# Two-layer decoder trunk on one core: the first FFN product in seven block products in place of eight, and layer 1's modulation vectors at other places

## The chip, the cores and the metric

The kernel runs on one core of a Trainium2 chip. The metric is the device time of one execution in microseconds (us); lower is better. One core has a matmul engine (TensorE, PE in the profile), two vector engines (VectorE or DVE, GpSimd or POOL), an activation engine (ScalarE, ACT), a sync engine (SyncE, SP) that here only issues transfers, and 16 DMA engines that move data between the chip's memory and the on-chip buffers.

## The reference, cut to what matters

```python
cond = jax.nn.silu(c)                                  # c: 1 x 1024
for layer in range(2):
    mod = cond @ ada_w[layer] + ada_b[layer]           # 1024 x 6144
    sh1, sc1, g1, sh2, sc2, g2 = jnp.split(mod, 6, axis=-1)
    h = modulate(rms_norm(x, mix_norm[layer]), sh1, sc1)
    y = ab_mixer(h, ...) if layer == 0 else cd_mixer(h, ...)
    x = x + g1[:, None, :] * y
    h = modulate(rms_norm(x, ffn_norm[layer]), sh2, sc2)
    gate, up = jnp.split(h @ w1[layer], 2, axis=-1)    # w1: 1024 x 5632
    x = x + g2[:, None, :] * ((silu(gate) * up) @ w2[layer])    # w2: 2816 x 1024
```

x has 512 tokens of 1024 features. The six modulation vectors of a layer (1024 numbers each) are numbered s0 to s5 in the kernel, in the order of the split; `ada_w` holds 4 MB for each. They don't depend on x, so they can be made at any time before they are used.

## The kernel before, in words

**Precision.** Every big product takes both operands as a sum of a rounded part hi and a rest lo and makes three matmuls, hi·hi, hi·lo, lo·hi (`mm3`, L119 to L122). `split` (L115) makes hi on ACT (L116) and lo on DVE (L117); in the mixers `lo_eng` may set lo on POOL.

**FFN, first product (`ffn`, L1226).** The 5632 columns of w1 are 22 gate tiles and 22 up tiles of 128 columns. For each i from 2 to 21 PE multiplies gate tile i and up tile i with all 512 tokens (8 row blocks × 3 matmuls of 128x512 each, called f), then `glu` (L1233) makes silu on ACT and the product g on DVE. Tiles 0 and 1 are multiplied earlier in `ffn_first` (L1205) in halves of 256 tokens. Weights come in 1 MB transfers into `rawp` (two buffers of 1 MB), 256 columns at a time (`load_cols`).

**FFN, second product.** For each i from 0 to 21, `kt(i)` (L1243) splits one tile of w2 (128x1024, two tiles per 1 MB transfer, `load_rows`, L410) and one tile of g; then PE makes 24 matmuls of 128x512 (called w) into the eight PSUM banks. The last four i's are made per block of 128 tokens, each followed by its gated residual.

**Modulation.** There are three ways to make a vector. `ada_strip` (L227): PE multiplies strips of `ada_w` with cond and `ada_cols` (L242) turns the row into columns. `ada_vec` (L255): 1 MB transfers into `adap` (one buffer of 1 MB), and DVE accumulates them with cond as a per-partition scalar, four operations on 128x512 per transfer (L217, L219). `ada_pair` (L278): the same for two vectors at once, 64 partitions each, in two transfers of 0.5 MB (L289), accumulated at L295 and L297 and finished by `pair_fin` (L299). In layer 0's first product the kernel makes s5 of layer 0, the pair s0, s1 of layer 1 and s2 of layer 1, one step for each i (`side`, `next(side, None)`); in layer 0's second product it makes the pair s3, s4 of layer 1, one step for every second i (`side2`). Each step issues the next transfer and accumulates the one issued a step before. Layer 1's first product makes s5 of layer 1. `gate_bcast` (L338) spreads a gate vector over all partitions by PE; for the FFN it stands at the end of the first product.

**Order.** PE, ACT, DVE and POOL execute in the order in which the code is written (`manual_schedule` with `MANUAL`); SP issues its transfers in program order, each when its buffer is free. In the mixers, generators are interleaved step by step by `run` (L517). In layer 1's mixer `in_cd` loads w_in with `load_cols` (L397) and `load_rows` (L410) into the two `rawp` buffers.

Of the kernel before, what the change touches and what calls it, by code (L numbers as in the profile page):

```python
# [69 lines left out]
def trunk(ctx, tc, x, c, positions, ada_w, ada_b, ffn_w1, ffn_w2, ab_w_in, gla_gate_up,  # L70
# [9 lines left out]
    adap = ctx.enter_context(tc.tile_pool(name="adap", bufs=1))  # L80
# [22 lines left out]
    def small(w=1, name="t"):  # L103
        return tiny.tile([P, w], F32, tag=f"t{w}", name=nm(name))

# [97 lines left out]
    def ada_acc(dst, rt, q, E):  # L203
        if E is G:
            r3 = rt.rearrange("p (j n) -> p j n", j=4)
            E.tensor_tensor(r3, r3, cond[:, 4 * q:4 * q + 4].unsqueeze(2).to_broadcast([P, 4, 512]), op=ALU.mult)
            E.tensor_tensor(rt[:, 0:1024], rt[:, 0:1024], rt[:, 1024:2048], op=ALU.add)
            if q:
                E.tensor_tensor(dst, dst, rt[:, 0:512], op=ALU.add)
                E.tensor_tensor(dst, dst, rt[:, 512:1024], op=ALU.add)  # L210
            else:
                E.tensor_tensor(dst, rt[:, 0:512], rt[:, 512:1024], op=ALU.add)
            return
        for j in range(4):
            r, c_ = rt[:, j * 512:(j + 1) * 512], cond[:, 4 * q + j:4 * q + j + 1]
            if q + j == 0:
                E.tensor_scalar(dst, r, c_, None, ALU.mult)  # L217
            else:
                E.scalar_tensor_tensor(dst, r, c_, dst, ALU.mult, ALU.add)  # L219

# [6 lines left out]
    def ada_strip(l, s, acc2, lag):  # L227
        src = ada_w[l].rearrange("(p j) n -> p j n", j=8)
        for n in range(2):
            acc = slot(name="acc")  # L230
            for q in range(2):
                rt = adap.tile([P, 2048], F32, tag="ada", name=nm("ada")).rearrange("p (j n) -> p j n", j=8)
                c0 = s * D + n * 512 + q * 256
                tc.keep_in_program_order(nc.sync.dma_start(rt, src[:, :, c0:c0 + 256]))
                for _ in range(lag):
                    yield
                ps = bank("ad")
                ada_mm(ps[:, 0:256], [rt[:, j] for j in range(8)], 0, 8)
                act(acc[:, q * 256:(q + 1) * 256], ps[:, 0:256], AF.Copy)
            acc2.append(acc)  # L240
# [14 lines left out]
    def ada_vec(l, s, acc2, E, lag):  # L255
        for n in range(2):
            acc2.append(slot(name="acc"))
            if s in (2, 5):
                b = slot(w=512, name="abrow")
                nc.scalar.dma_start(b[0:1], ada_b[l:l + 1, s * D + n * 512:s * D + (n + 1) * 512])  # L260
            for q in range(2):
                c0 = s * D + n * 512
                rt = adap.tile([P, 2048], F32, tag="ada", name=nm("ada"))
                ld = nc.sync.dma_start(
                    rt.rearrange("p (j n) -> p j n", j=4),
                    ada_w[l].rearrange("(p j) n -> p j n", j=8)[:, 4 * q:4 * q + 4, c0:c0 + 512])
                tc.keep_in_program_order(ld)
                for _ in range(lag):
                    yield
                ada_acc(acc2[n], rt, q, E)  # L270
            if s in (2, 5):
                E.tensor_tensor(acc2[n][0:1], acc2[n][0:1], b[0:1], op=ALU.add)
                hi, lo = slot(F32R, name="acchi"), slot(F32R, name="acclo")
                E.tensor_copy(hi, acc2[n])
                E.tensor_tensor(lo, acc2[n], hi, op=ALU.subtract)
                acc2[n] = hi, lo

    def ada_pair(l, s0, acc2):  # L278

        src = ada_w[l].rearrange("(p j) n -> p j n", j=16)  # L280
        for n in range(2):
            dst = slot(name="acc")
            acc2.append(dst)
            for q in range(4):
                rt = adap.tile([P, 2048], F32, tag="ada", name=nm("ada"))
                r3 = rt.rearrange("p (j n) -> p j n", j=4)
                for v in range(2):
                    c0 = (s0 + v) * D + n * 512
                    ld = nc.sync.dma_start(r3[64 * v:64 * v + 64], src[:, 4 * q:4 * q + 4, c0:c0 + 512])  # L289
                    tc.keep_in_program_order(ld)  # L290
                yield
                for j in range(4):
                    c_ = cond2[:, 4 * q + j:4 * q + j + 1]
                    if q + j == 0:
                        V.tensor_scalar(dst, r3[:, j], c_, None, ALU.mult)  # L295
                    else:
                        V.scalar_tensor_tensor(dst, r3[:, j], c_, dst, ALU.mult, ALU.add)  # L297
# [13 lines left out]
    def after(g, n, fn):  # L311
        for i, _ in enumerate(g):
            if i == n:
                fn()
            yield

# [4 lines left out]

    def ada_seq(l, ss, store, fin, E=None, lag=1):
        prev = []
        for s in ss:
            store[s] = []
            for i, _ in enumerate(ada_vec(l, s, store[s], E or V, lag)):
                if i == 2:
                    for q in prev:
                        ada_fin(l, q, store[q])
                    prev = []  # L330
                yield
            if fin and s not in (2, 5):
                prev = [s]
        if prev:
            yield
            ada_fin(l, prev[0], store[prev[0]])
# [1241 lines left out]
```

## Time and profile before

| quantity | value |
|---|---|
| three runs | 1246.60, 1246.76, 1250.62 us; median 1246.76 |
| profiled execution | 1251.88 us, its span 1250.1 us, mean granted clock 0.99 |
| busy over the span | PE 98%, DVE 55%, ACT 38%, POOL 12% |
| chain that ended last | PE 90%, DVE 5%, ACT 2%, issue 2% |
| layer 0, first product, tiles 2 to 21 | about 360.2 to 579.8 us |
| layer 0, second product, i from 0 to 17 | about 580.7 to 678.7 us |
| layer 1, mixer with its output product | about 709 to 881 us |

The span is the time from the first to the last recorded instruction; the profiled execution took 1.78 us more, and 5.12 us more than the median of the runs. The chain follows the end of the kernel back from releaser to releaser; its shares add up to the span. A granted clock of 1.00 in a stretch is 2.4 GHz.

### The profile page before, as it was taken

The numbers are of one execution on the slowest core, as the hardware profiler recorded it, in microseconds if no ns is written. First come the engines' busy times: TensorE is split into PE (matmuls) and PEld (weight loads), VectorE is DVE, ScalarE is ACT, GpSimd is POOL, SyncE is SP. The second block draws the span as 40 slices with busy tenths as digits, with TensorE's granted clock in tenths as the row PEclk, the third lists the DMA queues.
The fourth block names the chain that finished last, engine by engine and source line by source line (L and its number), as shares of the span: only waits on it lengthen the run. The fifth ranks groups of instructions, "written<-read, shape, count | busy, mean of one in ns | idle before, by whom it ended". The sixth has DMA issues, their size and how long they took to land.

```text
span 1250.1 us, 15248 instructions
## 1 busy us (share of the span) xinstructions
PE 1221.9 (98%) x5999; PEld 994.0 (80%) x6000; DVE 693.2 (55%) x1197; ACT 472.5 (38%) x917; POOL 153.0 (12%) x153
## 2 busy tenths in 40 slices
PE   7998999999999999999999999999999999999998
PEld 3776767878888888888888888787988888888886
DVE  4477789657744555654564727866736322224334
ACT  4356337645442122223222565643522222223330
POOL 2043135500100000000000174230100000000000
PEclk8998999999999999999999999999999999999999
DMA  9544554321144686736773123122335332432211
GB/s 314 202 135 134 174 169 136 117 103 40 39 159 135 190 214 162 237 116 185 200 197 114 68 68 110 34 68 68 102 109 195 97 105 69 134 101 101 101 68 68
DMA packets 106804, 160.62 MB, mean 128 GB/s; under 512 B 5334, under 2 KB 67814, under 8 KB 106732
## 3 DMA queue, kind: packets, MB, share of 16 engines
q1 hardware_dynamic: 104704, 158.71, 40.1%
q10 hardware_dynamic: 1964, 0.93, 0.3%
q8 instruction: 47, 0.77, 0.3%
q14 instruction: 25, 0.20, 0.1%
q0 software_dynamic: 64, 0.01, 0.0%
HBM read 157.53 MB, written 2.10 MB: 128 GB/s over the span
## 4 chain that ended last, share of the span: by engine, by line
PE 90%; DVE 5%; ACT 2%; issue 2%; DMA 1%; POOL 1%; ACTq 0%; SPq 0%; POOLq 0%; DVEq 0%
PE f L120 16%; PE f L121 16%; PE f L122 16%; PE w L121 6%; PE w L122 6%; PE w L120 6%; PE op L121 2%; PE op L122 2%; PE op L120 2%; PE ad L225 2%; PE f L128 1%; PE f L129 1%; PE f L131 1%; PE tp L378 1%; PE ko L647 1%
## 5 line engine op out<-in xcount | busy, mean ns | idle before, releaser
L116 ACT ACTIVATE whi<-raw 128x1024 fp32r<-128x1024 f32 x188 | 197.9, 1059 | 375.3 <-PE w L122 134.0
L120 PE MATMUL f<-hhi,whi 128*128 128x512 f32 (+1 forms) x704 | 267.3, 380 | 0.0
L121 PE MATMUL f<-hlo,whi 128*128 128x512 f32 (+1 forms) x704 | 267.2, 380 | 0.0
L122 PE MATMUL f<-hhi,wlo 128*128 128x512 f32 (+1 forms) x704 | 267.2, 380 | 0.0
L117 DVE TENSOR_TENSOR wlo<-raw,whi 128x1024 fp32r<-128x1024 f32 x148 | 178.0, 1222 | 137.0 <-ACT whi L116 136.9
L1236 DVE TENSOR_TENSOR g<-silu,f 128x512 f32<-128x512 f32 x44 | 30.3, 688 | 237.3 <-PE f L122 235.9
L120 PEld LDWEIGHTS f<-hhi,whi 128*128 128x128 f32 x704 | 132.5, 188 | 25.0
L122 PEld LDWEIGHTS f<-hhi,wlo 128*128 128x128 f32 x704 | 132.4, 188 | 24.8
L121 PEld LDWEIGHTS f<-hlo,whi 128*128 128x128 f32 x704 | 132.5, 188 | 24.8
L121 PE MATMUL w<-wlo,ghi 128*128 128x512 f32 x352 | 137.2, 390 | 0.3
L120 PE MATMUL w<-whi,ghi 128*128 128x512 f32 x352 | 137.2, 390 | 0.0
L122 PE MATMUL w<-whi,glo 128*128 128x512 f32 x352 | 137.0, 389 | 0.0
L117 POOL TENSOR_TENSOR wlo<-raw,whi 128x1024 fp32r<-128x1024 f32 x40 | 97.5, 2446 | 157.7 <-ACT whi L116 132.8
L120 PE MATMUL f<-whi,hhi 128*128 128x512 f32 x240 | 97.0, 404 | 1.8 <-DVE iqr L728 1.8
L121 PE MATMUL f<-wlo,hhi 128*128 128x512 f32 x240 | 95.2, 397 | 0.1
L122 PE MATMUL f<-whi,hlo 128*128 128x512 f32 x240 | 94.8, 395 | 0.0
L1235 ACT ACTIVATE silu<-f 128x512 f32<-128x512 f32 x44 | 26.2, 595 | 137.1 <-PE f L122 137.1
L121 PEld LDWEIGHTS w<-wlo,ghi 128*128 128x128 f32 x352 | 66.1, 188 | 14.6 <-DVE wlo L117 1.1
L122 PEld LDWEIGHTS w<-whi,glo 128*128 128x128 f32 x352 | 66.1, 188 | 13.8
L120 PEld LDWEIGHTS w<-whi,ghi 128*128 128x128 f32 x352 | 66.1, 188 | 13.7
L358 POOL TENSOR_TENSOR r<-ss 128x1 f32<-128x1 f32 x16 | 5.4, 338 | 498.5 <-ACT junk L356 498.4
L120 PEld LDWEIGHTS f<-whi,hhi 128*128 128x128 f32 x240 | 46.0, 192 | 15.7 <-issue 2.9
(296 smaller groups left out, 1786.1 us busy)
## 6 DMA issues: line engine op xcount, KB each, us to landing
raw<-in_ffn_w_dram SPq DMA_DIRECT2D x66, 1024.0 KB, 6.0
ada<-in_ada_w_dram SPq DMA_DIRECT2D x25, 1024.0 KB, 5.6
ada<-in_ada_w_dram SPq DMA_DIRECT2D x32, 512.0 KB, 6.5
raw<-in_ab_w_in_dram SPq DMA_DIRECT2D x12, 1024.0 KB, 5.5
raw<-in_cd_w_in_dram SPq DMA_DIRECT2D x8, 1024.0 KB, 6.3
ar<-in_ada_w_dram SPq DMA_DIRECT2D x20, 256.0 KB, 5.4
x<-in_x_dram SPq DMA_DIRECT2D x16, 256.0 KB, 5.8
raw<-in_ab_w_out_dram SPq DMA_DIRECT2D x4, 1024.0 KB, 5.0
```

The costliest lines, as they stand in the source:

```text
L116: act(hi, src, AF.Copy)
L117: lo_eng[0].tensor_tensor(lo, src, hi, op=ALU.subtract)
L120: mm(ps, ah, bh, start=first, stop=False)
L121: mm(ps, ah, bl, start=False, stop=False)
L122: mm(ps, al, bh, start=False, stop=last)
L128: mm(ps, ah, bh, start=i == 0, stop=False)
L129: mm(ps, *((ah, bl) if w_is_a else (al, bh)), start=False, stop=False)
L131: mm(ps, *((al, bh) if w_is_a else (ah, bl)), start=False, stop=i == n - 1)
L225: mm(ps[32 * g:32 * g + 32, :], condz[:, j, :], rows[j], start=j < 4, stop=j >= 4)
L378: nc.tensor.transpose(tp[:, i * P:(i + 1) * P], xn[k // 4][:, (k % 4) * P:(k % 4 + 1) * P], ident)
L1235: act(s, pg, AF.Silu)
L1236: V.tensor_tensor(gt[i], s, pu, op=ALU.mult)
```

## The change

**First product.** Tiles 0 to 3 (`NP = 4`) are multiplied as before. The other 18 are taken as nine groups q, each of gate tiles 4+2q and 5+2q and the up tiles of the same numbers. A group's product of 512 weight columns with 512 tokens over 1024 rows is cut into 2x2 blocks (gate and up, token halves of 256, row halves of 512), and seven block products in Winograd's order take the place of eight. Each block product (`step_mm`) is 2 column tiles × 4 row blocks × 3 matmuls of 128x256. Sums of h blocks are made once (`t_sums`), sums of weight blocks per group (`prep`, steps 0 to 3) and sums of products behind them (`post`). `prep(s + 3)` stands ahead of `step_mm(s)`. w1 comes in 1 MB pieces, 256 columns of gate or up (`q_load`), every third of them in two `adap` tiles.

**Modulation.** `adap` becomes two tiles of 0.5 MB. s5 of layer 0, the pair s0, s1 of layer 1 and s2 of layer 1 move into layer 0's second product: 8, 16 and 8 steps of one 0.5 MB tile, two steps for every i. The pair s3, s4 of layer 1 is dropped there and made in layer 1's mixer by `ada_strip`, eight strips, whose two 0.5 MB tiles each go through `adap`. `gate_bcast` and `pair_fin` of layer 0's FFN stand behind the matmuls of token block 0 of the tail, which copies its two sums out of PSUM first.

```diff
-    adap = ctx.enter_context(tc.tile_pool(name="adap", bufs=1))
+    adap = ctx.enter_context(tc.tile_pool(name="adap", bufs=2))
+    def ada_tile():
+        return adap.tile([P, 1024], F32, tag="ada", name=nm("ada"))
...
     def ada_pair(l, s0, acc2):
-            for q in range(4):
-                rt = adap.tile([P, 2048], F32, tag="ada", name=nm("ada"))
+            for q in range(8):
+                rt = ada_tile()
+                r3 = rt.rearrange("p (j n) -> p j n", j=2)
                 for v in range(2):
                     c0 = (s0 + v) * D + n * 512
+                    tc.keep_in_program_order(nc.sync.dma_start(
+                        r3[64 * v:64 * v + 64], src[:, 2 * q:2 * q + 2, c0:c0 + 512]))
                 yield
+                ada_acc(dst, rt, lambda j: cond2[:, 2 * q + j:2 * q + j + 1], q == 0)
...
+        def q_load(n):
+            c0 = (FF if n % 2 else 0) + (NP + n // 2 * 2) * P
+            if n % 3 == 2:
+                ts = [ada_tile().rearrange("p (k n) -> p k n", k=4) for _ in range(2)]
+                for r, t in enumerate(ts):
+                    nc.sync.dma_start(t, w1[512 * r:512 * r + 512, c0:c0 + 256].rearrange("(k p) n -> p k n", p=P))
+            else:
+                r3 = load_cols(w1, c0, 256)
+                ts = [r3[:, 0:4], r3[:, 4:8]]
+            raw[n] = ts
...
+        def prep(s):
...
+            if st == 0:
+                prep.x = gatep.tile([P, D], F32, tag="g", name=nm("s1")).rearrange("p (k n) -> p k n", k=4)
+                V.tensor_tensor(prep.x, a21, a22, op=ALU.add)
+            if st == 1:
+                prep.y = [slot(name="s2").rearrange("p (k n) -> p k n", k=4) for _ in range(2)]
+                for p in range(2):
+                    c_ = slice(p * P, (p + 1) * P)
+                    V.tensor_tensor(prep.y[p], prep.x[:, :, c_], a11[:, :, c_], op=ALU.subtract)
+            if st == 2:
+                V.tensor_tensor(a21, a11, a21, op=ALU.subtract)
+            if st == 3:
+                for p in range(2):
+                    V.tensor_tensor(prep.y[p], a12[:, :, p * P:(p + 1) * P], prep.y[p], op=ALU.subtract)
+            hi, lo = (t.rearrange("p (k n) -> p k n", k=4) for t in whl())
+            if st in (2, 6):
+                for p in range(2):
+                    c_ = slice(p * P, (p + 1) * P)
+                    split(hi[:, :, c_], lo[:, :, c_], prep.y[p])
+            else:
+                split(hi, lo, {0: a11, 1: a12, 3: a21, 4: prep.x, 5: a22}[st])
...
+            for p in range(2):
+                ps = cur[bk][:, p * 256:(p + 1) * 256]
+                c_ = slice(p * P, (p + 1) * P)
+                for k in range(4):
+                    bh, bl = moving(mv, k)
+                    mm(ps, hi[:, k, c_], bh, start=start and k == 0 and p == 0, stop=False, ...)
+                    mm(ps, hi[:, k, c_], bl, start=False, stop=False, ...)
+                    mm(ps, lo[:, k, c_], bh, start=False, stop=k == 3, ...)
...
+            elif st == 5:
+                V.tensor_tensor(ends["u2"], c_, ends["u2"], op=ALU.add)
+                V.tensor_tensor(ends["p7"], ends["u4"], ends["p7"], op=ALU.add)
...
-            for i in range(2, NF):
+            for i in range(2, NP):
...
+            for s in range(NS):
+                prep(s + 3)
+                step_mm(s)
+                post(s)
...
             for i in range(NF - NT_):
-                if i % 2 == 0:
-                    next(side2, None)
                 if i + 2 < NF:
                     kts.append(kt(i + 2))
                 for tb in range(NTB):
+                    if tb % 2 == 0:
+                        next(side2, None)
                     for n in range(2):
                         mmk(i, kts[i], tb, n)
...
-    side0b = ada_pair(1, 3, adap1)
+    side0 = chain(ada_vec(0, 5, ada0[5]), ada_pair(1, 0, adap0), ada_vec(1, 2, ada1[2]))
...
-    run(l1_main(), fin1(), delay(sbatt(), 6))
+    ad = chain(*(ada_strip(1, s_, ada1[s_], 1) for s_ in (3, 4)))
+    run(l1_main(), fin1(), delay(sbatt(), 6), keep=(ad,))
+    for _ in ad:
+        pass
+    for s_ in (3, 4):
+        ada_fin(1, s_, ada1[s_])
```

**Where the rows stand.** On PE, in the first product, one weight tile before is eight times three rows like these (hhi and hlo are h in its two parts, whi and wlo the weight tile; the number behind a name counts tiles).

```order
L120 MATMUL f_968_4058<-hhi_3131,whi_3972 128x512
L121 MATMUL f_968_4058<-hlo_3135,whi_3972 128x512
L122 MATMUL f_968_4058<-hhi_3131,wlo_3973 128x512
L120 MATMUL f_968_4058<-hhi_3131,whi_3972 128x512
L121 MATMUL f_968_4058<-hlo_3135,whi_3972 128x512
```

And after the change, inside one block product (its column tile ends with the second row):

```order
L1367 MATMUL f_962_4109<-hlo_3162,whi_4001 128x256
L1368 MATMUL f_962_4109<-hhi_3158,wlo_4002 128x256
L1365 MATMUL f_962_4109<-hhi_3157,whi_4001 128x256
L1367 MATMUL f_962_4109<-hlo_3161,whi_4001 128x256
L1368 MATMUL f_962_4109<-hhi_3157,wlo_4002 128x256
```

Matmuls of 512 columns gave way to matmuls of 256. A group of two gate and two up tiles had 4 × 24 = 96 matmuls of 512 columns and has 7 × 24 = 168 of 256 columns.

On DVE, in the middle of layer 0's second product, before (L117 is the lo part of a w2 tile or of g, L297 accumulates one pair tile of 1 MB):

```order
L117 TENSOR_TENSOR glo_5603<-g_3662,ghi_5602 128x512
L297 SCALAR_TENSOR_TENSOR acc_5414<-ada_5561,cond_87,acc_5414 128x512 x4
L117 TENSOR_TENSOR wlo_5640<-raw_5637,whi_5639 128x1024
L117 TENSOR_TENSOR glo_5644<-g_3663,ghi_5643 128x512
L117 TENSOR_TENSOR wlo_5672<-raw_5637,whi_5671 128x1024
L117 TENSOR_TENSOR glo_5676<-g_3664,ghi_5675 128x512
L297 SCALAR_TENSOR_TENSOR acc_5414<-ada_5634,cond_87,acc_5414 128x512 x4
```

And there after the change (L120 is the lo part, L249 accumulates one pair tile of 0.5 MB; e are the tiles of g that the block products leave):

```order
L120 TENSOR_TENSOR wlo_6233<-raw_6230,whi_6232 128x1024
L120 TENSOR_TENSOR glo_6237<-e_4366,ghi_6236 128x512
L120 TENSOR_TENSOR glo_6241<-e_4565,ghi_6240 128x512
L249 SCALAR_TENSOR_TENSOR acc_6159<-ada_6215,cond_87,acc_6159 128x512 x2
L249 SCALAR_TENSOR_TENSOR acc_6159<-ada_6246,cond_87,acc_6159 128x512 x2
L120 TENSOR_TENSOR wlo_6279<-raw_6230,whi_6278 128x1024
L249 SCALAR_TENSOR_TENSOR acc_6159<-ada_6263,cond_87,acc_6159 128x512 x2
L249 SCALAR_TENSOR_TENSOR acc_6159<-ada_6284,cond_87,acc_6159 128x512 x2
```

Between two lo parts of w2 there stand two accumulation steps of 0.5 MB now, where there was one step of 1 MB between every second pair.

On SP, in layer 1's mixer, the transfers before:

```order
L397 DMA raw_6555<-in_cd_w_in_dram 128x8x256
L397 DMA raw_6652<-in_cd_w_in_dram 128x8x256
L410 DMA raw_6865<-in_cd_w_in_dram 128x4x512
L410 DMA raw_6875<-in_cd_w_in_dram 128x4x512
L410 DMA raw_7188<-in_cd_w_out_dram 128x2x1024
```

And the same stretch after (L221 is a strip's tile, L369 and L382 are the loads of L397 and L410):

```order
L369 DMA raw_7580<-in_cd_w_in_dram 128x8x256
L369 DMA raw_7706<-in_cd_w_in_dram 128x8x256
L221 DMA ada_7399<-in_ada_w_dram 128x4x256
L221 DMA ada_7401<-in_ada_w_dram 128x4x256
L382 DMA raw_7948<-in_cd_w_in_dram 128x4x512
L221 DMA ada_7492<-in_ada_w_dram 128x4x256
L221 DMA ada_7494<-in_ada_w_dram 128x4x256
L221 DMA ada_7574<-in_ada_w_dram 128x4x256
L221 DMA ada_7576<-in_ada_w_dram 128x4x256
L382 DMA raw_7958<-in_cd_w_in_dram 128x4x512
L221 DMA ada_7632<-in_ada_w_dram 128x4x256
L221 DMA ada_7634<-in_ada_w_dram 128x4x256
```

The strips' transfers now stand between the weight transfers, that of the third strip (ada_7492, ada_7494) right behind raw_7948.

On PE, where the strip of ada_7492 and ada_7494 is multiplied after the change (tp are transposes of the attention, f is w_in times h):

```order
L1522 MATMUL tp_7550<-kt,sraw_7353 128x128 x4
L1522 MATMUL tp_7557<-kt,sraw_7374 128x128 x4
L210 MATMUL ad_7564<-ada_7492,condz 32x256 x4
L210 MATMUL ad_7564<-ada_7494,condz 32x256 x4
L131 MATMUL f_1530_7586<-hhi_6756,whi_7582 128x512
```

The strip's eight matmuls are new there; behind them on PE stands the mixer's main product.

## Rows read from the trace of the kernel before

**Rows 1.** The page: busy time by engine, and the chain that ended last.

```profile
PE 1221.9 (98%) x5999; PEld 994.0 (80%) x6000; DVE 693.2 (55%) x1197; ACT 472.5 (38%) x917; POOL 153.0 (12%) x153
...
PE 90%; DVE 5%; ACT 2%; issue 2%; DMA 1%; POOL 1%; ACTq 0%; SPq 0%; POOLq 0%; DVEq 0%
```

**Rows 2.** Windows: us, busy of PE, PEld, DVE, ACT, POOL, clock, DMA share, GB/s.

```profile
360.20:579.80 219.60, 219.60 (x979) 182.16 (x978) 112.80 (x139) 52.75 (x61) 0.00 (x0) 1.00 0.61 177
580.70:678.70 98.00, 98.00 (x434) 81.16 (x433) 58.14 (x71) 31.01 (x42) 0.00 (x0) 1.00 0.61 172
790.00:800.00 10.00, 8.01 (x33) 6.75 (x34) 9.06 (x21) 7.39 (x17) 1.39 (x3) 0.83 0.08 31
```

**Rows 3.** Timeline of PE, 560.14 to 574.87: first and last of 66 matmuls.

```profile
560.14 0.39 PE L121 MATMUL f<-hlo,whi 128*128 128x512 f32 x1
...
574.87 0.39 PE L120 MATMUL f<-hhi,whi 128*128 128x512 f32 x1
```

**Rows 4.** Timeline of PE, 348.64 to 351.88: first and last of 28 matmuls.

```profile
348.64 0.28 PE L120 MATMUL f<-hhi,whi 128*128 128x256 f32 x1
...
351.88 0.28 PE L120 MATMUL f<-hhi,whi 128*128 128x256 f32 x1
```

**Rows 5.** Groups of instructions, whole span: form, count, busy, mean ns, idle before.

```profile
L117 DVE TENSOR_TENSOR wlo<-raw,whi 128x1024 fp32r<-128x1024 f32 x148 | 178.0, 1222 | 137.0 <-ACT whi L116 136.9
L117 DVE TENSOR_TENSOR glo<-g,ghi 128x512 fp32r<-128x512 f32 x44 | 29.8, 685 | 0.0
L116 ACT ACTIVATE whi<-raw 128x1024 fp32r<-128x1024 f32 x188 | 197.9, 1059 | 375.3 <-PE w L122 134.0
L120 PEld LDWEIGHTS f<-hhi,whi 128*128 128x128 f32 x704 | 132.5, 188 | 25.0
```

**Rows 6.** Timeline of DVE in layer 0's second product, and two operations at 396 to 398.

```profile
592.75 1.23 DVE L117 TENSOR_TENSOR wlo<-raw,whi 128x1024 fp32r<-128x1024 f32 x1 [2.31 <-ACT whi L116]
...
606.59 3.12 DVE L297 SCALAR_TENSOR_TENSOR acc<-ada,cond,acc 128x512 f32<-128x512 f32 x4 [1.13 <-DMA ada<-in_ada_w_dram]
...
396.84 0.68 DVE L272 TENSOR_TENSOR acc<-acc,abrow 1x512 f32<-1x512 f32 x1
...
398.02 0.69 DVE L275 TENSOR_TENSOR acclo<-acc,acchi 128x512 fp32r<-128x512 f32 x1
```

**Rows 7.** Timeline of SP's queue in the same stretch.

```profile
599.11 1.26 SPq L289 DMA_DIRECT2D ada<-in_ada_w_dram  x2
```

**Rows 8.** DMA engines' busy tenths, 599.0 to 607.5 us in 40 slices, and their rate.

```profile
DMA  0100000896499999999999999988632059093799
GB/s 0 19 0 0 0 0 0 154 135 154 116 376 395 347 212 222 231 193 222 212 231 231 260 202 222 222 173 173 135 68 39 10 154 308 0 154 154 328 366 443
```

**Rows 9.** Tiles: ada at 340 to 415, ada at 560 to 700, raw at 580 to 680.

```profile
DMA to landing us min/median/max: 5.1/5.2/5.2
...
DMA to landing us min/median/max: 4.9/6.5/7.5
...
DMA to landing us min/median/max: 4.8/4.8/6.1
```

**Rows 10.** The chain in order of time: strips in layer 0's mixer, columns at 732, transposes.

```profile
111.27 1.00 PE ad L225 x16
...
732.16 1.68 PE ac L302 x16
...
753.06 0.88 PE tp L1360 x8
```

**Rows 11.** Timeline of SP's queue in layer 1's mixer.

```profile
749.50 9.17 SPq L410 DMA_DIRECT2D raw<-in_cd_w_in_dram  x2
767.85 0.37 SPq L410 DMA_DIRECT2D raw<-in_cd_w_out_dram  x1
```

**Rows 12.** Timeline of POOL at 747, and of PE at 791, in layer 1's mixer.

```profile
747.07 2.40 POOL L117 TENSOR_TENSOR wlo<-raw,whi 128x1024 fp32r<-128x1024 f32 x1 [0.35 <-ACT whi L116]
...
791.92 0.33 PE L1468 MATMUL sn<-sphi,tri 128*128 128x128 f32 x1 [2.17 <-DVE mixlo L1526]
```

## What is predicted

> **What bounds the kernel now.** I read the page first: PE is busy 98% of the span and holds 90% of the chain that ended last [rows 1]. So only what PE executes, or waits for, sets the time. Then the stretches that the change touches: in the first product and in the second product of layer 0, PE is busy for the whole window at clock 1.00 [rows 2], while DVE has 112.8 of 219.6 us and 58.1 of 98.0 us. Every matmul taken away there shortens the end; every wait put in lengthens it. Layer 1's mixer is different: near its end PE has 8.01 of 10 us at clock 0.83 [rows 2], behind a wait for DVE of 2.17 us [rows 12].
>
> **1. The block products (a gain).** 66 matmuls of 512 columns lie between 560.14 and 574.87: 14.73 / 65 = 226.6 ns from start to start [rows 3]. 28 matmuls of 256 columns between 348.64 and 351.88 give 3.24 / 27 = 120.0 ns [rows 4]. The durations of 0.39 and 0.28 us in the rows overlap; the spacing is the cost. Per layer 18 tiles × 48 = 864 matmuls go, 864 × 226.6 = 195.8 us; 9 groups × 7 × 24 = 1512 come, 1512 × 120.0 = 181.4 us. That is -14.4 a layer, **-28.8** for two: one eighth of the work is saved (24.5 us), but a matmul of half the columns costs 53% of a whole one, which eats 10.1 of it. The break-even spacing is 195.8 / 1512 = 129.5 ns.
>
> The Trainium skill (TensorE: Matmul & The Clock Gate, Back-to-back issue gap) speaks against the change: it gives sustained spacings, set by weight load and matmul together, of 81 ns at 128 and 131 ns at 512 columns, an estimate from it of 98 ns at 256. By it the change would cost 1512 × 98 - 864 × 131 = +35 us a layer. This case's rows show 120.0 and 226.6 ns, so the trace does not agree and the sum goes by the rows.
>
> The cover: one group gives PE 168 × 0.120 = 20.2 us. DVE has in it seven operations on 128x1024 (two sums and five lo parts; 1222 ns is the mean, of which some 80 overlap the next, so 1.14 each) and thirteen on 512 columns (four sums, four lo parts, five operations behind the products; 685 ns is the mean, about 0.60 each) [rows 5]: 8.0 + 7.8 = 15.8 us, under 20.2. ACT has five hi parts at 1.06 [rows 5], four halves and six copies or silus at about 0.6: 11.3. Work is prepared three block products ahead, 8.6 us. Nothing is added to the sum; without cover (a group over 195.8 / 9 = 21.8 us) the gain is gone.
>
> **2. Layer 0's second product (a loss).** One i gives PE 24 × 0.2266 = 5.44 us. DVE there has a lo part of w2 and one of g, 1.14 + 0.60, and now two accumulations of half a transfer, 2 × 1.56 (3.12 for the whole [rows 6]): 4.9 us. The gate vectors add 1.9 us (396.84 to 398.71 [rows 6]) per four tiles. DVE is thus close under PE and can't catch up much; what decides is how fast tiles arrive. Before, a pair tile of 1 MB was issued at 599.11 [rows 7] and accumulated at 606.59, after a wait of 1.13 us [rows 6]: 7.4 us. One tile was needed per 10.9 us, so it was hidden. Now four half tiles are needed in that time, 2 MB. Two buffers take turns: landing plus 1.56 us of DVE per two tiles, against 5.44. The landing of a half tile isn't in the trace. Its upper bound is the whole one's 7.4. In the rows the engines are at nine tenths for about 4.5 us of it at some 220 GB/s [rows 8], so 2.9 us are not transfer; half of 4.5 plus 2.9 is 5.1, my value; the lower bound is 3.7, half of all.
>
> So two pair tiles cost about 5.1 + 1.6 = 6.7, and four 13.4, where PE's two i's have 10.9. The w2 transfer (1 MB, 4.8 [rows 9]) shares the engines, but lies mostly in the gaps. There are four such groups of four: 4 × 2.5 to 3.2 = 10 to 13 us. Tiles over 128 partitions land in 5.2 as wholes [rows 9], half about 3.8, four in 2 × (3.8 + 1.6) = 10.8, with the gate's end some 0.7 more: 4 × 0.6 = 2.5 us in the two gate vectors. DVE executes in order, so a late tile also holds back the lo parts of w2 behind it, and those are two i's (10.9 us) ahead of PE at the best. A delay of 12.5 to 15.5 is thus lessened by what PE has in hand when it starts, about one i (5.4 us): **+9**, from 0 (a half tile lands in 3.7, 2 × 5.3 per four tiles, under 10.9) to 23 (it lands in 7.4, 2 × 9.0 per four, 4 × 7.1 us over, less 5.4).
>
> **3. Layer 1's mixer (a loss).** 16 strip matmuls take 1.00 us on PE [rows 10], so eight strips of eight take 4.0. Columns cost two times 1.68 in place of the pair's 1.68 [rows 10]: +1.7. Then the transfers: the third strip's two tiles stand on SP behind raw_7948, whose counterpart was issued at 749.50 [rows 11], because its buffer came free when POOL ended a lo part at 747.07 + 2.40 [rows 12]. Issued there, behind 1 MB, it lands at about 757; PE wants it behind the transposes that end at 753.94 [rows 10], so some 3.5 us of wait, with the mixer's main product queued behind it. The sixth stands so behind the counterpart of 767.85 [rows 11]: 1 to 2.4. Against it, up to 2.2 us fall into the wait at 791.92 [rows 12] that is there anyway. A wait of some us may also lower the clock as at 790 to 800, where ten us lost about 1.7. Together 4.0 + 1.7 + 3.5 + 1.2 - 2.2 = **+8**, from 4 (strips alone) to 12 (no absorption, a drop of the clock).
>
> **4. The rest.** `gate_bcast` moves behind token block 0's matmuls: two ACT copies of about 0.6 and two more residual operations wait, with the next blocks' matmuls behind them on PE in other banks: about +1, 0 to 2. The four accumulations that leave the first product were hidden there [rows 2].
>
> **Sum:** -28.8 + 9 + 8 + 1 = -11. Against the profiled execution 1251.9 - 11 = 1241. That execution lies 5.1 above the median of the runs, so the median comes to 1246.8 - 11 = **1236**.
>
> **The rivals.** A difference under 0.3%, 3.7 us, is about what a measurement here can't tell from no change.
> - *The tiles keep up in layer 0's second product.* For it: the engines' share is only 0.61 there [rows 2], and two half tiles are under way at once, so each landing hides behind the other. Against it: 7.4 us of before. Then term 2 falls to 0 to 2: 1246.8 - 28.8 + 8 + 1 = 1227. Chance 0.25.
> - *The tiles come late enough to take all back (the other side).* The mechanism: each pair tile is two transfers of 64 partitions; if it takes as long as before, 7.4 us, whatever its size, four tiles take 18 us. For it: a pair tile of two 0.5 MB transfers over 64 partitions each took longer than 1 MB over 128 (6.5 to 5.2 [rows 9]). Term 2 is then 18 to 23, the time 1245 to 1250, and above with the gate vectors' tiles late too. From 28.8 - 9 = 20 us of wait on it is slower than before. Chance 0.2.
> - *The block products don't hold 120 ns.* Those 28 matmuls last 3.2 us; the new stretch lasts 181. Each has a weight load of 188 ns [rows 5] which has to be hidden behind others. If DVE's preparation becomes the bound instead, it is at the same place. At 126 ns, 5% more, nothing but 10.6 is left of the gain: 1254. Against it: PE was never seen to wait for loads there. Chance 0.1. The Trainium skill's page named in part 1 (Back-to-back issue gap) is the rule of this rival; with its figures the time would be 1246.8 + 2 × 35 + 18 = 1335, and since both spacings in the rows differ from it, no chance is given to that size.
> - *As summed*: 0.45, with its own range of 1230 to 1243.
>
> **How the numbers follow.** Faster by over 0.3% means under 1243: the sum's case nearly whole (0.43), the first rival (0.25) and a little of the second (0.02), 0.70. Within 0.3%, up to 1250.5: most of the second and the sum's rest, 0.15. Slower: 0.15, from the second's end and the third. The range reaches from 1224 (tiles keep up, mixer at its lower bound) to 1251.
>
> **What would show it.** Term 1: the window of nine groups at 181 us, spacing 120 ns, no idle PE; wrong if PE waits there for wlo by DVE. Term 2: the stretch of the second product with PE idle, released by DVE's lo parts of w2, and these by accumulations that wait for ada; right if 9 us idle in 107, wrong if none. Term 3: PE idle before the strips at 753 and 770 of the old time, released by DMA ada. Wrong altogether if the clock falls below 1.00 in the block products, or if the sums at their start (seven on h, 22 us of DVE with the first splits) hold up the first group.

## The result, and the profile after

The changed kernel took 1262.02 us (median of four runs, 1258.64 to 1264.14) against 1246.86 for the kernel before: ratio 1.0112, 95% interval 1.0081 to 1.0143. It is slower, by 15 us, where 11 us of gain were forecast.

The page after, with the same parts as [rows 1]: busy time by engine, the chain that ended last by engine, and by line.

```profile
PE 1216.7 (96%) x7440; PEld 1040.9 (82%) x7440; DVE 875.9 (69%) x1450; ACT 580.1 (46%) x1107; POOL 155.1 (12%) x153
...
PE 81%; DMA 9%; DVE 6%; ACT 2%; issue 1%; POOL 1%; SPq 1%; ACTq 0%; DVEq 0%; POOLq 0%
PE f L1368 10%; PE f L1367 10%; PE f L1365 10%; DMA ada<-in_ada_w_dram 8%; PE f L123 5%; PE f L124 5%; PE f L125 5%; PE w L124 4%; PE w L125 4%; PE w L123 4%; PE op L123 2%; PE op L125 2%; PE op L124 2%; PE ad L210 2%; DVE acc L249 2%; PE f L131 1%
```

PE's share of the chain fell from 90 to 81%, and 8% of it, about 100 us, is now the loading of modulation tiles, where all of DMA was 1% before [rows 1]. To see where, I cut both traces at the start of the first matmul of each stage and of the last w (us, from the groups f of 256 columns and w on PE). The differences add up to 12.3 us, that of the two profiled executions' spans (1250.1 and 1262.4), not to the 15 of the medians.

| stage | before | after | difference |
|---|---|---|---|
| up to the first f of layer 0's FFN | 334.6 | 330.5 | -4.1 |
| layer 0, first product | 334.6 to 580.6 | 330.5 to 559.3 | -17.2 |
| layer 0, second product | 580.6 to 701.8 | 559.3 to 715.6 | +35.1 |
| layer 1, mixer | 701.8 to 881.2 | 715.6 to 907.2 | +12.2 |
| layer 1, first product | 881.2 to 1125.3 | 907.2 to 1135.9 | -15.4 |
| layer 1, second product, end | 1125.3 to 1250.1 | 1135.9 to 1262.4 | +1.7 |

The gain of the block products is there; the second product of layer 0 takes it back. Windows of the changed kernel, columns as in [rows 2]: the nine groups of block products, then the second product in three pieces.

```profile
377.60:559.30 181.70, 181.70 (x1515) 181.63 (x1514) 145.22 (x178) 95.34 (x136) 0.00 (x0) 1.00 0.34 107
...
559.30:640.00 80.70, 74.51 (x315) 59.41 (x313) 53.24 (x71) 21.89 (x29) 0.00 (x0) 0.98 0.69 198
640.00:692.00 52.00, 38.10 (x138) 28.75 (x139) 35.30 (x47) 10.13 (x14) 0.00 (x0) 0.87 0.65 198
692.00:716.50 24.50, 24.28 (x116) 19.93 (x115) 15.58 (x37) 9.86 (x21) 1.87 (x6) 0.93 0.08 31
```

In the first row PE has no gap in 181.70 us at clock 1.00. In the third it is busy 38.1 of 52 us at a granted clock of 0.87: it stands and, after standing, runs a while at the lower of its two levels. PE's rows after its longest wait show that level: they start 0.42 to 0.43 us apart, where 0.2266 was the spacing at clock 1.00 [rows 3].

```profile
687.15 0.63 PE L125 MATMUL w<-whi,glo 128*128 128x512 f32 x1
687.58 0.63 PE L123 MATMUL w<-whi,ghi 128*128 128x512 f32 x1
688.00 0.63 PE L124 MATMUL w<-wlo,ghi 128*128 128x512 f32 x1
```

The waits of PE from 559 to 700 name the releaser (us, times, longest):

```profile
PE w L124 <- DVE wlo L120: 19.8, 9, 5.5
```

DVE's lo parts of w2 come late. DVE's timeline at one such place shows why they do:

```profile
606.22 3.12 DVE L249 SCALAR_TENSOR_TENSOR acc<-ada,cond,acc 128x512 f32<-128x512 f32 x4 [3.37 <-DMA ada<-in_ada_w_dram]
609.25 1.22 DVE L120 TENSOR_TENSOR wlo<-raw,whi 128x1024 fp32r<-128x1024 f32 x1
612.50 1.54 DVE L249 SCALAR_TENSOR_TENSOR acc<-ada,cond,acc 128x512 f32<-128x512 f32 x2 [2.03 <-DMA ada<-in_ada_w_dram]
615.36 1.54 DVE L249 SCALAR_TENSOR_TENSOR acc<-ada,cond,acc 128x512 f32<-128x512 f32 x2 [1.32 <-DMA ada<-in_ada_w_dram]
616.82 1.22 DVE L120 TENSOR_TENSOR wlo<-raw,whi 128x1024 fp32r<-128x1024 f32 x1
```

The lo part at 609.25 waits for nothing of its own. It stands in DVE's order behind two accumulations, the first of which sat 3.37 us for its tile. The chain that ended last runs through these tiles from 575 to 685 us, and their landings alternate in it:

```profile
598.10 8.00 DMA ada<-in_ada_w_dram
...
608.44 3.94 DMA ada<-in_ada_w_dram
...
614.71 7.34 DMA ada<-in_ada_w_dram
...
624.38 3.85 DMA ada<-in_ada_w_dram
...
630.57 7.21 DMA ada<-in_ada_w_dram
...
646.18 7.98 DMA ada<-in_ada_w_dram
```

The long ones are the tiles that were issued just behind a w2 transfer, as the next lines show. SP's queue gives the period: one w2 transfer for every two i's and four half tiles.

```profile
579.95 0.37 SPq L382 DMA_DIRECT2D raw<-in_ffn_w_dram  x1
...
595.75 0.54 SPq L382 DMA_DIRECT2D raw<-in_ffn_w_dram  x1
...
610.66 0.59 SPq L382 DMA_DIRECT2D raw<-in_ffn_w_dram  x1
...
626.38 0.59 SPq L382 DMA_DIRECT2D raw<-in_ffn_w_dram  x1
...
642.29 0.59 SPq L382 DMA_DIRECT2D raw<-in_ffn_w_dram  x1
...
658.17 0.37 SPq L382 DMA_DIRECT2D raw<-in_ffn_w_dram  x1
...
673.02 0.37 SPq L382 DMA_DIRECT2D raw<-in_ffn_w_dram  x1
```

That is 14.8 to 15.9 us per two i's, where PE wants 10.9, and about as slow for the gate vectors (accumulated before 592 and from 656 on) as for the pair.

### The profile page after: what moved, and what is told of

Same layout as the page of the kernel before. It is cut to its first block, busy times and chain, and to the rows that moved or that the text cites. A ratio compares the mean times of both kernels' runs of the same rounds, so it can differ in the third digit from the quotient of the medians.

```text
span 1262.4 us, 18783 instructions
## 1 busy us (share of the span) xinstructions
PE 1216.7 (96%) x7440; PEld 1040.9 (82%) x7440; DVE 875.9 (69%) x1450; ACT 580.1 (46%) x1107; POOL 155.1 (12%) x153
## 4 chain that ended last, share of the span: by engine, by line
PE 81%; DMA 9%; DVE 6%; ACT 2%; issue 1%; POOL 1%; SPq 1%; ACTq 0%; DVEq 0%; POOLq 0%
PE f L1368 10%; PE f L1367 10%; PE f L1365 10%; DMA ada<-in_ada_w_dram 8%; PE f L123 5%; PE f L124 5%; PE f L125 5%; PE w L124 4%; PE w L125 4%; PE w L123 4%; PE op L123 2%; PE op L125 2%; PE op L124 2%; PE ad L210 2%; DVE acc L249 2%; PE f L131 1%
## 5 line engine op out<-in xcount | busy, mean ns | idle before, releaser
L120 DVE TENSOR_TENSOR wlo<-raw,whi 128x1024 fp32r<-128x1024 f32 x124 | 151.0, 1221 | 83.0 <-ACT whi L119 83.0
L1367 PE MATMUL f<-hlo,whi 128*128 128x256 f32 x576 | 163.0, 283 | 0.0
L1368 PE MATMUL f<-hhi,wlo 128*128 128x256 f32 x576 | 163.0, 283 | 0.0
L1365 PE MATMUL f<-hhi,whi 128*128 128x256 f32 x576 | 163.0, 283 | 0.0
L124 PE MATMUL w<-wlo,ghi 128*128 128x512 f32 x352 | 141.8, 403 | 19.9 <-DVE wlo L120 19.8
L1365 PE MATMUL f<-thi,whi 128*128 128x256 f32 x432 | 122.3, 283 | 0.0
L1367 PE MATMUL f<-tlo,whi 128*128 128x256 f32 x432 | 122.3, 283 | 0.0
L1368 PE MATMUL f<-thi,wlo 128*128 128x256 f32 x432 | 122.3, 283 | 0.0
L120 POOL TENSOR_TENSOR wlo<-raw,whi 128x1024 fp32r<-128x1024 f32 x40 | 97.5, 2446 | 161.2 <-ACT whi L119 133.3
L1372 ACT ACTIVATE e<-f 128x512 f32<-128x512 f32 x90 | 53.8, 597 | 131.5 <-PE f L1368 131.5
L120 DVE TENSOR_TENSOR wlo<-s,whi 128x512 fp32r<-128x512 f32 (+1 forms) x90 | 68.5, 794 | 45.1 <-ACT whi L119 45.1
L249 DVE SCALAR_TENSOR_TENSOR acc<-ada,cond,acc 128x512 f32<-128x512 f32 x72 | 54.1, 752 | 46.6 <-DMA ada<-in_ada_w_dram 45.0
```

The source lines that it names most:

```text
L120: lo_eng[0].tensor_tensor(lo, src, hi, op=ALU.subtract)
L124: mm(ps, ah, bl, start=False, stop=False)
L249: V.scalar_tensor_tensor(dst, r3[:, j], col(j), dst, ALU.mult, ALU.add)
L1365: mm(ps, hi[:, k, c_], bh, start=start and k == 0 and p == 0, stop=False, skip_group_check=not start or p == 1)
L1367: mm(ps, hi[:, k, c_], bl, start=False, stop=False, skip_group_check=not start or p == 1)
L1368: mm(ps, lo[:, k, c_], bh, start=False, stop=k == 3, skip_group_check=not start or p == 1)
```

## The experiments

Three theories of the second product's 35.1 us were open: A, landing and accumulation in turn through two buffers; B, the DMA engines' throughput; C, DVE's own work. The stretch below is always the first to the last w of layer 0 on PE (121.2 us before, 156.3 after; the expectations below have 121.7 for the first, to the start of another w). The kernel before was run again beside every experiment and its median moved between 1246.86 and 1249.84 us, so a difference between two experiments' times can be off by up to 3 us; the stages are read within one trace each.

**Four tiles in place of two.**

```diff
-HEAP = 52
+HEAP = 48
-    adap = ctx.enter_context(tc.tile_pool(name="adap", bufs=2))
+    adap = ctx.enter_context(tc.tile_pool(name="adap", bufs=4))
```

> The changed kernel with four modulation tiles of 0.5 MB in place of two (and four temporaries fewer, which pay for the room). Layer 0's second product, first to last matmul, took 121.7 us before and 156.3 after the change. Theory A, each load waits for one of two buffers and lands too late: with four in flight the stretch falls to about 127 to 130 us, the time to 1236. Theory B, the DMA engines can't move 3.1 MB per two i's (2 MB of modulation, 1 MB of w2) in 10.9 us however many are in flight: the stretch stays over 145 us, the time within 5 us of 1262.

Measured: 1244.60 us, ratio to before 0.9963 (0.9946 to 0.9980); the stretch is 136.7 us. It lies between the theories: 19.6 us come back, so buffers are part of it, and 10.6 us more than without loads (next run) remain. The tiles' landing, pair tiles alone, at the source line of their loads, in this run:

```profile
L282 SPq DMA_DIRECT2D ada<-in_ada_w_dram x32: 595/598/1764, 578.1 to 633.9; - x32
...
DMA to landing us min/median/max: 3.5/8.0/10.2
```

With four in flight the median landing is 8.0 us, yet no accumulation waits for a tile in this run from 560 to 690. What holds the pair's part back is a fourth cause that the theories do not name, the place of the w2 transfer in SP's order. The chain of this run:

```profile
602.97 0.60 SPq L282
603.66 9.41 DMA raw<-in_ffn_w_dram
613.17 1.07 ACT whi L119
614.27 1.11 DVE wlo L120
615.41 1.29 DVE glo L120 x2
616.70 0.67 DVE acc L249
...
618.82 0.61 SPq L282
619.52 8.66 DMA raw<-in_ffn_w_dram
```

DVE's timeline at the lo part in it:

```profile
614.27 1.23 DVE L120 TENSOR_TENSOR wlo<-raw,whi 128x1024 fp32r<-128x1024 f32 x1 [6.24 <-ACT whi L119]
```

SP issues the w2 transfer behind eight transfers of tiles (L282), the last of which wait until DVE frees a buffer. The w2 transfer then takes 9.41 us, ACT waits for it and DVE for ACT, and the accumulation that frees the next buffer stands behind that lo part. So w2 is issued every 15.1 to 16.3 us in the pair's part (587.40, 603.66, 619.52, 634.62), about as slowly as with two buffers, and every 4.8 to 13.4 us behind it, in the gate vectors. No run tests this by issuing w2 earlier.

**Modulation tiles loaded once.**

```diff
             for q in range(4):
-                rt = ada_tile()
-                tc.keep_in_program_order(nc.sync.dma_start(...))
+                if q == 0:
+                    rt = ada_tile()
+                    tc.keep_in_program_order(nc.sync.dma_start(...))
...
```

> Leaves out three of four (seven of eight for the pair) loads of the modulation vectors that VectorE makes in the second products; VectorE accumulates the same tile again, so its work stays. If the loads are what delays layer 0's second product (theories A and B), the stretch falls from 156 to about 125 us (121.7 and 3.3 for the gate that moved there) and the time to 1231. Theory C, VectorE's own work there (two accumulations, one or two lo parts per i, in order) is the limit: the stretch stays over 140 us, the time over 1246.

Measured: 1233.85 us, 0.9876 (0.9857 to 0.9895); the stretch is 126.1 us, without a wait for DVE. DVE does all its accumulations there, so C alone does not make the delay. 30.2 of the 35.1 us are the loads'; the other 4.9 are the gate's matmuls and the pair's columns that moved in (3.3 us on PE) and a clock of 0.93 in the tail, as after.

**w2 loaded once.**

```diff
-            if i % 2 == 0 and i:
+            if l and i % 2 == 0 and i:
                 kt_load(i)
```

> The changed kernel, two modulation tiles; leaves out ten of the eleven w2 transfers of layer 0 (VectorE and ScalarE split the first one again, so their work stays). The 2 MB of modulation per two i's remain. Theory A (landing and accumulation in turn through two buffers): the loop of two tiles still takes landing plus 1.56 us; with the landing of a tile that shares the engines with less (4 to 5.1 us) the stretch is 134 to 142 us, the time 1240 to 1248. Theory B (engines' throughput for modulation and w2 together): 2 MB in 10.9 us are 193 GB/s, which they move; the stretch falls to 126 as without the modulation's loads, the time to 1232.

Measured: 1241.51 us, 0.9943 (0.9922 to 0.9963); the stretch is 132.6 us. Between the theories again. The landing of the pair's half tiles, in the changed kernel and then in this run:

```profile
L282 SPq DMA_DIRECT2D ada<-in_ada_w_dram x32: 595/602/1228, 584.0 to 646.2; - x32
...
DMA to landing us min/median/max: 3.3/5.8/8.1
```

```profile
L282 SPq DMA_DIRECT2D ada<-in_ada_w_dram x32: 595/599/729, 580.2 to 629.2; - x32
...
DMA to landing us min/median/max: 3.4/3.6/4.3
```

Without w2 a transfer of a half tile lands in 3.6 us. In the changed kernel the median of 5.8 mixes two sizes, 3.8 to 3.9 and 7.2 to 8.0 on the chain, the latter beside w2. The pair's 16 tiles (two transfers of 0.25 MB each) were issued over 62.2 us after the change and over 49.0 here: some 8.2 and 6.5 us per two tiles. A and B are thus no alternatives: w2 lengthens the landing, and two buffers pass each lengthened landing on to DVE. (w2's own landing does not stand on the changed kernel's chain from 575 to 685, as it does with four tiles.) Taking away either most of the sharing (23.7 us) or the wait for two buffers (19.6 us) brings most of it back.

**No strips in the mixer.**

```diff
-    ad = chain(*(ada_strip(1, s_, ada1[s_], 1) for s_ in (3, 4)))
-    run(l1_main(), fin1(), delay(sbatt(), 6), keep=(ad,))
...
+    run(l1_main(), fin1(), delay(sbatt(), 6))
+    V.tensor_copy(adaT[:, 1, 24:40], prmT[:, 72:88])
+    ada_amul(1, 1)
```

> Leaves out the eight strips in layer 1's mixer (their loads, their 64 matmuls, the columns); shift and scale of layer 1's FFN are taken from the biases alone. By the stages the mixer grew by 12.2 us: the time should fall to 1250. By the prediction's term it falls by 8, to 1254. Rival, the growth is a shift of waits that were there anyway and the strips cost little more than their 4 us on PE: 1258.

Measured: 1246.93 us, 0.9981 (0.9968 to 0.9993), 15.1 under the changed kernel; the mixer is 177.7 us in place of 191.6. The strips and their columns cost 13.9 there, which is the whole growth of 12.2 and the 1.7 of the pair's columns that were dropped.

**Strips loaded once.**

```diff
-                    rt = ada_tile().rearrange("p (j n) -> p j n", j=4)
-                    tc.keep_in_program_order(nc.sync.dma_start(...))
-                    rows += [rt[:, j] for j in range(4)]
+                    if l == 0 or len(strip1) < 8:
+                        rt = ada_tile().rearrange("p (j n) -> p j n", j=4)
+                        tc.keep_in_program_order(nc.sync.dma_start(...))
+                        rows += [rt[:, j] for j in range(4)]
+                if l:
+                    strip1.extend(rows)
+                    rows = strip1
```

> Leaves out seven of the eight strips' loads in layer 1's mixer and multiplies the first strip eight times; PE's work is all there. Without strips the stretch from the last w of layer 0 to layer 1's block products was 13.7 us shorter and the time 15. If the price is PE's own work (eight strips of 16 matmul records, 1.00 us each, and the columns), the time falls by no more than 3 us, to 1259. If it is the waits for late loads and what they bring after them (the prediction gave waits and clock 4.7 of its 8 us), by 6 or more, to 1256 or below.

Measured: 1259.70 us, 1.0085 (1.0068 to 1.0103), 2.3 under the changed kernel; the mixer is 188.5 us. The time is within what two experiments can differ by, so the stage counts: 3.1 of the 13.9 us go with the late loads and 10.8 stay with PE's own work. The chain of the changed kernel shows one strip, and the rows of the tile ad on PE, from 740 to 830, all of them:

```profile
752.44 1.00 PE ad L210 x16
```

```profile
L210 PE MATMUL ad<-ada,condz x128: 376/379/403, 752.4 to 817.4; 128*32 128x256 f32 x128
```

Each strip is eight matmuls in the code, 16 in the records: eight strips take 8.0 us of PE, and the columns of the two vectors 3.8 (878.43 to 882.22). Part of that falls into a wait that was there before: the one of 2.17 us [rows 12] is 0.7 after the change.

**The modulation's move alone (no block products).**

```diff
-    NP = 4
+    NP = NF
...
-                    for n in range(3):
-                        q_load(n)
                 else:
+                    kt_load(0)
...
```

> The changed kernel with all 22 tiles of the first product multiplied whole, as before the change; the modulation stays where the change put it. If the block products give what the prediction's first term says, this is 28.8 us slower than the changed kernel: 1291. By the two stages (16.7 and 15.4 us shorter, 3.3 of it the gate that moved out of layer 0's): also 1291. Rival, the block products' load on VectorE and the transfers is part of what delays the second product: less than 25 us slower, since the second product recovers.

Measured: 1290.48 us, 1.0334 (1.0314 to 1.0355): 28.5 us slower than the changed kernel. By the two ratios to the kernel before it is 27.7. The second product is 155.1 us here, so all but 1.2 us of its delay is there without the block products.

**The steps spread over both products.** The w1 pieces get a third buffer of their own (`rawp` 3, `HEAP` 48), which frees the modulation tiles in the first product.

```diff
             for s in range(NS):
                 prep(s + 3)
                 step_mm(s)
                 post(s)
+                if s % 7 in (1, 4):
+                    next(side2, None)
...
-                    if tb % 2 == 0:
+                    if tb == 0:
                         next(side2, None)
...
```

> All work stays; only the place of the modulation steps in layer 0 changes. A third 1 MB weight buffer (paid with four temporaries) takes the w1 pieces that went through the modulation tiles, so that steps can run in the first product: two per group of block products, 18 of 32, the pair first; the other 14 in the second product, one per i. Loads that come too fast are then the cause no more: the second product 126 to 128 us as without loads, the first product unchanged (VectorE at 95% of it instead of 79%), the time 1232. Rival: VectorE becomes the bound of the block products (they have 4.2 us to spare per group, two steps take 3.1 and the ends of a vector more): the first product grows by 10 us or more, the time 1242 or above.

Measured: 1235.99 us, 0.9889 (0.9863 to 0.9915). The stretch is 126.2 us, and the window 380 to 562 in the block products has no idle PE, with DVE busy 165 of 182 us. The same 32 steps cost nothing where they don't come faster than one per i.

**Back to VectorE, the last nine steps in the mixer.** As the spread version, with `ada_pair(1, 3, adap1)` behind the others and no strips.

> As the spread version, and the pair s3, s4 of layer 1 goes back from PE's strips to VectorE's accumulation: 16 more steps behind the other 32, of which 18 run in the first product, 21 in the second, and the last 9 in layer 1's mixer, one per step of its main work. If the strips' price of 13.7 us is mostly PE's, this gives 10 to 13 us on top of the spread version: 1220. Rival: VectorE, which PE waits for in that mixer, gives it back there: 1230 or above.

Measured: 1228.03 us, 0.9838 (0.9805 to 0.9871). The mixer is 183.9 us, 7.4 less than in the spread version, not 10 to 13: PE waits there 3.4 and 2.9 us for DVE.

**All 48 steps in the two products, 30 of them in the second.**

> The spread version's 18 steps in the first product, and the pair s3, s4 made by VectorE as before the change: 48 steps, the other 30 in layer 0's second product (1.67 per i, against 0.78 in the spread version and 1.78 in the changed kernel), none and no strips in the mixer. By the account from the runs (with w2 beside them four half tiles take 15.7 us where two i's take 10.9) 30 tiles take 118 us in place of 98, less the i in hand: the second product comes back to 138 to 142 us, the mixer falls from 191 to 179, the time is 1236 to 1240. Rival, two steps per i were harmful only with the gate vectors among them or by their number: the second product stays under 130, the time 1224 to 1228.

Measured: 1243.21 us, 0.9950 (0.9932 to 0.9968). The stretch is 146.8 us, with 15.7 us of waits for DVE: at 1.67 steps per i the delay is back, and larger than I had counted from the changed kernel's rate. The third buffer of the spread version is there too, so it is not what cured the delay there.

**All 48, three per group in the first product.**

```diff
-                if s % 7 in (1, 4):
+                if s % 7 in (1, 3, 5):
...
```

> As the run before, but three steps per group of block products: 27 of the 48 in the first product, 21 in the second. VectorE then has 15.8 + 3 × 1.56 = 20.5 us of work per group of 20.2 us. If its time is counted rightly, the block products grow by 3 to 5 us, the second product stays at 126, the mixer is at 179: 1226 to 1229. Rival, VectorE is harmless since the first steps of each group have slack: no growth, 1223. Other rival, in-order waits make it worse: the first product grows by 10 us or more, the time 1234 or above.

Measured: 1228.26 us, 0.9833 (0.9811 to 0.9855). Windows from 380 to 562 in the block products and from 562 to 660 in the second product:

```profile
380.00:562.00 182.00, 178.60 (x1483) 177.85 (x1482) 170.92 (x223) 93.92 (x135) 0.00 (x0) 1.00 0.64 178
562.00:660.00 98.00, 98.00 (x444) 81.53 (x443) 75.89 (x102) 30.96 (x40) 0.00 (x0) 1.00 0.73 230
```

PE loses 3.4 us, as counted, though not to a late weight part itself. The releaser is ACT (us, times, longest):

```profile
PE f L1359 <- ACT e L1366: 3.4, 3, 2.2
```

These are ACT's copies of products out of PSUM. They stand in ACT's order behind hi parts that wait for DVE's sums, by up to 5.7 us in this stretch. In the second row the engines move 230 GB/s, more than the 198 of the changed kernel, and PE never waits. So there is no ceiling at 200 GB/s that theory B could have meant. The mixer is back at 179.0 us. This version and the one with the last nine steps in the mixer beat both kernels, by about 20 us against the kernel before and 34 against the changed one.

## Why the prediction was wrong

**Term 1, the block products, was right.** -28.8 forecast, 28.5 measured by taking them away (27.7 by the ratios). The spacing held over 181 us: 1515 records in 181.70 us are 119.9 ns, with a weight load for each, which disposes of the third rival. The Trainium skill's spacings beside that rival (TensorE: Matmul & The Clock Gate, Back-to-back issue gap) would put 256 columns at an estimated 98 ns; the trace does not agree over the whole stretch either. DVE had 145.2 / 9 = 16.1 us of work per group (15.8 forecast), ACT 10.6 (11.3).

**Term 2, the second product, is the step that failed**: +9 forecast with a bound of 23, 30.2 measured for the loads alone. The mechanism was right in its outline: two buffers in turn, DVE in order, lo parts behind late tiles. What failed in it is the premise on w2, and with it the time per four tiles.
- "The w2 transfer (1 MB, 4.8) shares the engines, but lies mostly in the gaps." It does not: on the chain every second tile lands beside it, in 7.2 to 8.0 us against 3.8 to 3.9, and w2 itself lands in 9.3 (median of the raw tiles from 575 to 670) in place of 4.8 [rows 9]. A round of four pair tiles took 15.6 to 16.6 us (from 598.10 to 614.71, 630.57 and 646.18 on the chain), where 13.4 were forecast. Without w2 two tiles took 6.5 us, close to the forecast's 6.7, and that run had 6.5 us left over 126.1, near the forecast's 9. The demand was in reach of the rows: 2 MB and 1 MB in 10.9 us are some 290 GB/s. In the longest run of nine tenths in [rows 8] the engines moved 193 to 395, in the changed kernel 198 over the stretch, and no run moved more than 230 over the main part of this product.
- The gate vectors' tiles were priced at 10.8 per four and 0.7 for the vector's end, since they lie over 128 partitions. The period of SP's w2 transfers is 14.8 there: their four groups were late by nearly as much as the pair's, not by 0.6.

With these two periods the prediction's own sum is 4 × (16.0 - 10.9) + 4 × (14.8 - 10.9) - 5.4 = 30.6, an estimate beside the 30.2 measured.

The granted clock was left out of this term, and for the most part rightly. PE's waits sum to 19.8 us. From 640 to 692 its 138 matmuls kept it busy 38.1 us, 6.8 more than at 0.2266 each. But up to 685 the chain runs through the tiles and DVE, so a slower PE there only waits less. After PE's last wait, at 686.6, the lower clock does lengthen the end: by some 2 us for the 15 matmuls up to 692 (an estimate, 5.4 us against 15 × 0.2266).

The range's upper end stood on the landing of 7.4 in the pair's four groups; with all eight groups the same bound would have given 51. The rival on the other side named the place and the outcome, at too low a price, and the chance of 0.15 for slower was too small. Its mechanism is not what happened: it had every tile take 7.4 us whatever its size, while a half tile lands in 3.6 to 3.9 where no w2 transfer is under way.

**Term 3, the mixer, was mis-sized**: +8 forecast, 12.2 in the stages, 13.9 by taking the strips away. "16 strip matmuls take 1.00 us on PE, so eight strips of eight take 4.0": the row of 16 was one strip, as the strips of layer 0 in the same chain were [rows 10]. PE's work is 8.0 and not 4.0. The columns were 3.8 where the prediction had 3.4. The waits were 3.1 us, where 4.7 had been counted, less 2.2.

**Term 4** was small: the gate and the pair's columns are 3.3 us of PE in layer 0's second product now, and layer 1's second product grew by 1.7 with its gate. The first products are shorter by the matmuls that left them, and a cost of its own is not to be seen.

By the measured terms, -28.5 + 30.2 + 12.2 = +14, against 15 measured.

What stays open: the stage up to layer 0's FFN was 4.1 us shorter in the profiled execution, but its end scatters over some 4 us among the experiments, whose code there is the same, so I give it to none of the edits. And the 10.6 us that four tiles leave over the run without loads are read from that run's chain, as w2 behind the tiles on SP; no run shows what w2 issued ahead of them would give.

## What to carry to other kernels

When loads move into a stage, put everything that the stage loads in one period side by side before pricing any single landing: a transfer's landing depends on what is in flight with it (here 3.6 to 3.9 us or 7.2 to 8.0). Look also at the order of the queue: a weight transfer behind loads that wait for their buffers starts only when those are freed. Work that fills idle engines is best put where it comes at the slowest rate; the same 32 steps cost 30 us at two per i, and nothing with 18 of them in the first product and 14 at one per i. Count matmul records, not calls in the code, before multiplying a row.

## What the runs showed of the hardware

A transfer of 0.25 MB, half of a modulation tile, landed in 3.6 us (median) where only its own kind was in flight, two tiles at a time. Just behind a 1 MB transfer the pair's tiles landed in 7.2 to 8.0 us on the changed kernel's chain, at 198 GB/s over the stretch, and with four tiles and w2 in flight the median was 8.0. The same engines moved 230 GB/s over 98 us in the last run without a wait of PE. The granted clock, 1.00 through 181.7 us of 256-column matmuls without a gap, fell to 0.87 on average over 52 us in which PE stood 13.9 us in pieces of at most 5.5 us; after the longest, matmuls of 512 columns started 0.42 to 0.43 us apart in place of 0.2266. With VectorE busy 94% of the time (170.9 of 182 us) in the block products, PE lost 3.4 us to copies on ScalarE that stood behind VectorE's late sums.
